# Decoder layer on one core: every SBUF tile starts on a multiple of 128 bytes

## Chip, core and metric

The kernel runs on one core of one Trainium2 chip. The metric is the device time of one execution in microseconds (us); what is compared is the median of several runs. TensorE (PE in the profile) does the matrix products, VectorE (DVE), ScalarE (ACT) and GpSimd (POOL) the elementwise work, and SyncE (SP) issues most of the transfers (DMA).

## The reference

One layer of a decoder, 1024 tokens by 1024 features, all in float32:

```
n   = RMSNorm(h)
c_q, c_kv, k_pe, q_sb, k_sb, v_sb, gate_a, gate_b = split(n @ w_in)
o_a = latent attention from c_q, c_kv, k_pe    (8 heads, rotary part, causal softmax)
o_b = stick-breaking attention(q_sb, k_sb, v_sb)                 (8 heads, causal)
h  += (sigmoid(gate_a) * (o_a @ w_br_mla) + sigmoid(gate_b) * (o_b @ w_br_sb)) @ w_out
n2  = RMSNorm(h)
h  += (silu(n2 @ w_ffn_gate) * (n2 @ w_ffn_up)) @ w_ffn_down     (inner width 2816)
h  += sigmoid(h @ w_ple_gate) * RMSNorm(p @ w_ple_proj)
out = RMSNorm(h)
```

## The kernel before

Each factor of a product is split into two float32r tiles, a high part and the rest (`split`, L115: a cast on ScalarE, a subtraction on VectorE), and a product is three passes, high by high, high by rest, rest by high (`passes`, L119 to L124). Each pass is one matmul with its own load of weights (PEld): `lhsT` is loaded as the weights, `rhs`, 512 columns of 2,048 bytes per partition, streams past them as the moving operand. The profile names a product by its PSUM tile:

- `nb` (L327): the value projection, up to 100 us. `pt` (L203, L354, L385, L393): query, key, low-rank and gate projections. Some stand in the first 100 us; the rest fill the stick-breaking attention (100 to 480 us) and are there till about 560.
- latent attention to 820 us; `pb` (L766) and `po` (L775), the merge and the output product, to about 960.
- `pP`, `pQ`, `pR` (L927): the gate and up products of the feed-forward, 22 units of seven products of 12 passes (a Strassen-like scheme, `wino`, L896), from about 960 to 1490 us. The work around a unit: SP loads `raw` (1 MB), POOL forms sums (L901, L902, L918, L920) and multiplies gate by up (L966), VectorE subtracts (L959), SP stores the results to DRAM (L956), loads four blocks of `w_ffn_down` into `t` tiles (L1077), VectorE adds them in pairs (L1080), SP stores the sums (L1081) and loads the next `raw`. SP issues in the order in which these stand. Two `embed` steps (L1028) lie between.
- `pd` (L1153): the down product, 1490 to 1710 us; `pg` (L1194): the last gate, then the output.

A scheduler sets the order of the instructions on each engine; a tile's slot is reused when its readers have finished.

**Where tiles lie.** SBUF pools are stacks, one from the left end, one from the right, and the framework gives each tile a whole number of 32-byte slots. The left stack begins on a multiple of 128 bytes; the small constants (L90 to L101) take 32 or 96 bytes each, in all a multiple of 128, so the large left tiles start on such a multiple, except those behind other small tiles. The right stack ends at 229,344 bytes, which is 96 past a multiple of 128, so its tiles start 96 bytes past one, or, below a pool with small tiles, 32. For the large products the start of the operands, modulo 128 bytes, is, read off the built program:

| product | weights | at | moving operand | at |
|---|---|---|---|---|
| nb | nTh, nTl | 96 | w_h, w_l | 32 |
| pt | w_h, w_l | 32 | nTh, nTl | 96 |
| pP, pQ, pR | wl (both parts) | 96 | b | 0 |
| pb (L766) | wh, wl | 96 | oh, ol | 96 |
| po | wo | 0 | mT | 0 |
| pd | dls | 32 | drs | 32 |
| pg | wpg | 0 | hs | 0 |

Every slice that a pass takes starts a multiple of 512 bytes into its tile, so these numbers hold for each pass.

Of the kernel before, what the change touches and what calls it, by code (L numbers as in the profile page):

```python
# [10 lines left out]
F32 = mybir.dt.float32  # L11
# [8 lines left out]
P = 128  # L20
S = 1024
D = 1024
NT = S // P
NK = D // P
# [27 lines left out]
def decoder_layer(ctx: ExitStack, tc: tile.TileContext, x, p, positions, g_mix, w_in, g_q_a, w_q_b,  # L52
                  g_kv_a, w_kv_b, w_br_mla, w_br_sb, w_out, g_ffn, w_ffn_gate, w_ffn_up, w_ffn_down,
                  w_ple_gate, w_ple_proj, g_ple, g_final, xT, pT, out):
    nc = tc.nc
# [6 lines left out]
    def pool(stack, name, side="left", space=None, bufs=1):  # L62
        kw = {} if space is None else {"space": space}
        if space is None:
            kw["side"] = side
        return stack.enter_context(tc.tile_pool(name=name, bufs=bufs, reuse_waits="tile", **kw))

    dram = ctx.enter_context(tc.tile_pool(name="dram", bufs=1, space=DRAM))
    d_c = dram.tile([Q_RANK + KV_RANK + 2 * ROPE, S], F32, name="d_c")
# [9 lines left out]
    d_rope = dram.tile([64, S], F32, name="d_rope")  # L79


    const = pool(ctx, "const", side="left")
    ident = const.tile([P, P], F32, name="ident")
    make_identity(nc, ident)
    atc = ExitStack()
    attc = pool(atc, "attconst")
    ident_r = attc.tile([P, P], F32R, name="ident_r")
    nc.vector.tensor_copy(out=ident_r, in_=ident)

    mhalf = const.tile([P, 1], F32, name="mhalf")  # L90
    nc.vector.memset(mhalf, -0.5)

    ones = const.tile([P, 1], F32, name="ones")
    nc.vector.memset(ones, 1.0)
    ones_pp = const.tile([P, P], F32, name="ones_pp")
    nc.vector.memset(ones_pp, 1.0)
    gains = const.tile([P, 3, NK], F32, name="gains")
    for gi, g in enumerate((g_ffn, g_ple, g_final)):
        nc.sync.dma_start(out=gains[:, gi, :], in_=g.rearrange("o (k p) -> p (o k)", p=P))
    r_ple = const.tile([P, NT], F32, name="r_ple")  # L100
    r_ffn = const.tile([P, NT], F32, name="r_ffn")  # L101
    incl = attc.tile([P, P], F32R, name="incl")
    rest = attc.tile([P, P], F32R, name="rest")
    mask_sb = attc.tile([P, P], F32R, name="mask_sb")
# [36 lines left out]
    late = ExitStack()  # L141
    with ExitStack() as att:
        ps = pool(ctx, "psum", space=PSUM)
        A = dict(tag="A", bufs=4)
        B = dict(tag="B", bufs=2)
# [14 lines left out]
        with ExitStack() as sb:  # L160
# [63 lines left out]
            with ExitStack() as p0:  # L224
# [13 lines left out]
                for t in range(NT):  # L238
# [8 lines left out]
                    for c in range(0, NK, 4):  # L247
                        tp = ps.tile([P, 512], F32, name="tp", **(B if c == 0 else A))
# [23 lines left out]
            with ExitStack() as p2:  # L272
                rp = pool(p2, "ropetab", side="left")

                HI = slice(64, 128)
                gcol = const.tile([P, 5], F32, name="gcol")
                nc.sync.dma_start(out=gcol[:, 0:3], in_=g_q_a.rearrange("o (k p) -> p (o k)", p=P))
                nc.sync.dma_start(out=gcol[:, 3:5], in_=g_kv_a.rearrange("o (k p) -> p (o k)", p=P))
                frow = rp.tile([1, 64], F32, name="frow")
                for i in range(16):  # L280
                    for j, sg in enumerate((1.0, 1.0, -1.0, 1.0)):
                        nc.gpsimd.memset(frow[0:1, 16 * j + i:16 * j + i + 1], sg * INV_FREQ[i])
                fcol = rp.tile([P, 2], F32, name="fcol")
                nc.sync.dma_start(out=d_freq, in_=frow)
                nc.sync.dma_start(out=fcol[HI, 0:1], in_=d_freq.rearrange("o f -> f o"))
                nc.gpsimd.memset(fcol[64:96, 1:2], math.pi / 2)
                nc.gpsimd.memset(fcol[96:128, 1:2], 0.0)
                pos_i = rp.tile([P, S], I32, name="pos_i")
                nc.sync.dma_start(out=pos_i[HI, :], in_=positions.broadcast_to([64, S]))
                ang = rp.tile([P, S], F32, name="ang")  # L290
                kk = rp.tile([P, S], F32, name="kk")
                kh = rp.tile([P, S], F32, name="kh")
                an, k_, h_ = ang[HI], kk[HI], kh[HI]
                V = nc.vector
                V.tensor_copy(out=k_, in_=pos_i[HI, :])
                V.tensor_scalar(out=an, in0=k_, scalar1=fcol[HI, 0:1], scalar2=None, op0=ALU.mult)
                V.tensor_scalar(out=k_, in0=an, scalar1=1.0 / (2 * math.pi), scalar2=None, op0=ALU.mult)
                V.tensor_scalar(out=k_, in0=k_, scalar1=MAGIC, scalar2=None, op0=ALU.add)
                V.tensor_scalar(out=k_, in0=k_, scalar1=-MAGIC, scalar2=None, op0=ALU.add)
                V.tensor_scalar(out=h_, in0=k_, scalar1=1.0 / 4096.0, scalar2=None, op0=ALU.mult)  # L300
                V.tensor_scalar(out=h_, in0=h_, scalar1=MAGIC, scalar2=None, op0=ALU.add)
                V.tensor_scalar(out=h_, in0=h_, scalar1=-MAGIC, scalar2=None, op0=ALU.add)
                V.scalar_tensor_tensor(out=k_, in0=h_, scalar=-4096.0, in1=k_, op0=ALU.mult, op1=ALU.add)
                for c in TWO_PI_PARTS:
                    V.scalar_tensor_tensor(out=an, in0=h_, scalar=-4096.0 * c, in1=an, op0=ALU.mult, op1=ALU.add)
                    V.scalar_tensor_tensor(out=an, in0=k_, scalar=-c, in1=an, op0=ALU.mult, op1=ALU.add)
                V.tensor_scalar(out=an, in0=an, scalar1=fcol[HI, 1:2], scalar2=None, op0=ALU.add)
                V.tensor_scalar(out=k_, in0=an, scalar1=math.pi, scalar2=-2.0 * math.pi, op0=ALU.is_gt, op1=ALU.mult)
                V.tensor_tensor(out=an, in0=an, in1=k_, op=ALU.add)
                V.tensor_scalar(out=an, in0=an, scalar1=PI_BELOW, scalar2=-PI_BELOW, op0=ALU.min, op1=ALU.max)  # L310
                nc.scalar.activation(out=an, in_=an, func=AF.Sin)
                nc.sync.dma_start(out=d_rope, in_=an)
# [171 lines left out]
        with ExitStack() as ml:  # L484
# [64 lines left out]
            for c in range(3):  # L549
                t = wk.tile([P, S], F32, name="cq", tag="pw1", bufs=4)  # L550
# [128 lines left out]
            for h in range(HEADS):  # L679
# [17 lines left out]
                if h == 5:  # L697
# [8 lines left out]
                        oa.append(hl)  # L706
                    oa.append([oah, oal])
    atc.close()

    bigs = itertools.cycle((M, A, A, A, A))  # L710

# [411 lines left out]
    for i in (1, 2, 6, 5, 7, 3, 4):  # L1123
# [31 lines left out]
        f, t = {1: (0, 0), 2: (0, 0), 6: (0, 1), 5: (1, 1), 7: (1, 1), 3: (0, 1), 4: (1, 0)}[i]  # L1155
# [93 lines left out]
```

## Time and profile before

| | |
|---|---|
| median of 3 runs | 1819.79 us (1817.94 to 1823.07) |
| the profiled execution's own time | 1825.25 us |
| its span, first to last instruction | 1823.5 us |
| PE busy | 1725.6 us (95%), 8148 matmuls |
| DVE, ACT, POOL busy | 1185.3, 907.0, 373.1 us (65%, 50%, 20%) |
| mean granted TensorE clock | 0.978 |
| chain that ended last, by engine | PE 70%, DVE 10%, DMA 7%, issue 6%, POOL 3%, ACT 2% |

Busy time of PE says little here: ends of matmuls are modelled, and one that lasts 0.39 us by the record overlaps the next. The spacing of their starts tells the pace. The chain is followed back from the last instruction, at each step to what released it; what an engine does beside the chain is hidden. The granted clock is 1.00 at 2.4 GHz and 0.5 at 1.2 GHz.

### The profile page before, as it was taken

How to read it: one execution, taken by the hardware profiler on the slowest of the kernel's cores; microseconds unless marked ns; L12 is line 12 of the kernel's file. 1: busy time of each engine (PE TensorE's matmuls, PEld its weight loads, DVE VectorE, ACT ScalarE, POOL GpSimd, SP SyncE). 2: the span in 40 equal slices, each digit the busy share in tenths (PEclk: the TensorE clock that was granted, in tenths of full speed). 3: DMA queues.
4: the chain of work that ended last, by engine and by line, in shares of the span. 5: the costliest groups of instructions: out<-in, count | busy, mean ns of one | idle time of the engine just before them, and what ended most of it. 6: DMA issues, size and time to landing. Idle time of an engine off the chain costs nothing.

```text
span 1823.5 us, 23396 instructions
## 1 busy us (share of the span) xinstructions
PE 1725.6 (95%) x8148; PEld 1416.5 (78%) x8148; DVE 1185.3 (65%) x2077; ACT 907.0 (50%) x1762; POOL 373.1 (20%) x401
## 2 busy tenths in 40 slices
PE   6999999999999999996997999989999999999996
PEld 5888878888787888875885777768778778887795
DVE  6666788777886667776569666654642455556655
ACT  5265677766765767765234433343333334445421
POOL 2011210000212433333104133324313410000000
PEclk9999999999999999998998999999998999999998
DMA  5212122213314111218840266464523328665522
GB/s 168 57 56 51 52 59 59 64 47 99 104 47 151 54 59 36 64 59 321 295 154 32 88 204 201 172 213 165 194 91 106 110 87 311 192 191 171 168 69 77
DMA packets 172345, 223.21 MB, mean 122 GB/s; under 512 B 23426, under 2 KB 104322, under 8 KB 172226
## 3 DMA queue, kind: packets, MB, share of 16 engines
q1 hardware_dynamic: 166194, 201.78, 34.4%
q0 software_dynamic: 6032, 19.93, 3.0%
q8 instruction: 64, 1.05, 0.3%
q14 instruction: 55, 0.45, 0.1%
HBM read 152.98 MB, written 67.90 MB: 121 GB/s over the span
## 4 chain that ended last, share of the span: by engine, by line
PE 70%; DVE 10%; DMA 7%; issue 6%; POOL 3%; ACT 2%; SPq 1%; DVEq 0%; POOLq 0%; ACTq 0%
PE pt L122 5%; PE pt L123 5%; PE pt L124 5%; PE pd L122 4%; PE pd L123 4%; PE pd L124 4%; DMA t<-w_ffn_down 2%; PE pP L124 2%; PE pP L122 2%; PE pP L123 2%; PE tp L636 2%; DVE t L959 2%; PE pg L124 1%; PE po L122 1%; PE pg L123 1%
## 5 line engine op out<-in xcount | busy, mean ns | idle before, releaser
L122 PE MATMUL pt<-nTh,w_h 128*128 128x512 f32 (+1 forms) x480 | 192.4, 402 | 3.3 <-ACT go L340 2.3
L117 DVE TENSOR_TENSOR wl<-raw,wl 128x512 fp32r<-128x512 f32 x132 | 112.1, 849 | 122.5 <-ACT wl L116 122.1
L123 PE MATMUL pt<-nTl,w_h 128*128 128x512 f32 (+1 forms) x480 | 190.2, 396 | 0.0
L124 PE MATMUL pt<-nTh,w_l 128*128 128x512 f32 (+1 forms) x480 | 189.5, 396 | 0.0
L124 PE MATMUL pP<-b,wl 128*128 128x512 f32 x352 | 142.5, 407 | 13.0 <-DVE wl L117 13.0
L116 ACT CAST wl<-raw 128x512 fp32r<-128x512 f32 x132 | 82.0, 621 | 138.3 <-PE pP L124 63.3
L122 PE MATMUL pP<-b,wl 128*128 128x512 f32 x352 | 143.3, 407 | 4.2 <-ACT wl L116 2.6
L123 PE MATMUL pP<-b,wl 128*128 128x512 f32 x352 | 142.1, 404 | 0.0
L122 PEld LDWEIGHTS pt<-nTh,w_h 128*128 128x128 f32 (+1 forms) x480 | 90.0, 188 | 26.1 <-ACT go L340 5.0
L124 PEld LDWEIGHTS pt<-nTh,w_l 128*128 128x128 f32 (+1 forms) x480 | 90.2, 188 | 20.4
L123 PEld LDWEIGHTS pt<-nTl,w_h 128*128 128x128 f32 (+1 forms) x480 | 90.2, 188 | 19.2
L123 PE MATMUL pd<-drs,dls 128*128 128x512 f32 x296 | 102.1, 389 | 1.0 <-DVE drs L117 1.0
L124 PE MATMUL pd<-drs,dls 128*128 128x512 f32 x296 | 102.0, 389 | 0.0
L117 DVE TENSOR_TENSOR drs<-drr,drs 128x512 fp32r<-128x512 f32 x74 | 50.9, 690 | 77.3 <-ACT drs L116 77.3
L122 PE MATMUL pd<-drs,dls 128*128 128x512 f32 x296 | 99.6, 392 | 0.4 <-ACT dls L116 0.4
L116 ACT CAST drs<-drr 128x512 fp32r<-128x512 f32 x74 | 45.9, 623 | 101.6 <-PE pd L124 99.1
L124 PEld LDWEIGHTS pP<-b,wl 128*128 128x128 f32 x352 | 68.2, 194 | 33.2 <-DVE wl L117 16.9
L622 POOL TENSOR_SCALAR pw<-pw,st 128x128 f32<-128x128 f32 (+5 forms) x48 | 74.9, 1567 | 71.7 <-DVE st L618 20.4
L122 PEld LDWEIGHTS pP<-b,wl 128*128 128x128 f32 x352 | 68.1, 194 | 22.6 <-ACT wl L116 4.1
L123 PEld LDWEIGHTS pP<-b,wl 128*128 128x128 f32 x352 | 67.7, 192 | 16.0
L430 DVE TENSOR_TENSOR sz<-sz,T 128x512 f32<-128x512 f32 (+2 forms) x96 | 52.2, 550 | 36.1 <-PE T L428 35.0
L122 PE MATMUL pQ<-b,wl 128*128 128x512 f32 x176 | 70.4, 401 | 1.3 <-ACT b L116 0.8
(373 smaller groups left out, 4793.6 us busy)
## 6 DMA issues: line engine op xcount, KB each, us to landing
d_g<-t SPq DMA_DIRECT2D x74, 256.0 KB, 2.1
drr<-d_g SPq DMA_DIRECT2D x74, 256.0 KB, 2.9
w_raw<-w_in SPq DMA_DIRECT2D x33, 512.0 KB, 4.3
raw<-w_ffn_gate SPq DMA_DIRECT2D x11, 1024.0 KB, 5.4
raw<-w_ffn_up SPq DMA_DIRECT2D x11, 1024.0 KB, 6.7
t<-w_ffn_down SPq DMA_DIRECT2D x44, 256.0 KB, 4.2
d_w<-t SPq DMA_DIRECT2D x44, 256.0 KB, 2.2
drr<-d_w SPq DMA_DIRECT2D x44, 256.0 KB, 2.7
```

Source lines behind the costliest of these rows:

```text
L116: nc.scalar.copy(out=h, in_=src)
L117: eng.tensor_tensor(out=l, in0=src, in1=r32(h), op=ALU.subtract)
L122: nc.tensor.matmul(ps, lhsT=ah, rhs=bh, start=first and i == 0, stop=False, **kw)
L123: nc.tensor.matmul(ps, lhsT=ah, rhs=bl, start=False, stop=False, **kw)
L124: nc.tensor.matmul(ps, lhsT=al, rhs=bh, start=False, stop=last and i == n - 1, **kw)
L430: nc.vector.tensor_tensor(out=sz[:, c0:], in0=sz[:, c0:], in1=T[:, c0:], op=ALU.subtract)
L622: nc.gpsimd.tensor_scalar(out=pw[:, 0:nk], in0=pw[:, 0:nk], scalar1=st[:, 6:7], scalar2=None, op0=ALU.mult)
L636: nc.tensor.transpose(tp[:, i * P:(i + 1) * P], rows[i][:, kb * P:(kb + 1) * P], ident)
L959: nc.vector.tensor_tensor(out=dst, in0=a, in1=b, op=ALU.subtract)
```

## The change

In every SBUF pool a tile whose bytes per partition are no multiple of 128 is padded to the next multiple (class `Lines`; the kernel works on the unpadded view). The small constants go into one tile `cols` of 256 bytes. A tile of 96 bytes, never used, is put at the right edge first, so that all later right-hand tiles start on a multiple of 128. `ones_pp`, the matrix of ones for the broadcasts of L721, moves from the constants to a pool that opens once the attention constants are closed, in the place of one of them.

```diff
-        return stack.enter_context(tc.tile_pool(name=name, bufs=bufs, reuse_waits="tile", **kw))
+        tp = stack.enter_context(tc.tile_pool(name=name, bufs=bufs, reuse_waits="tile", **kw))
+        return tp if space is not None else Lines(tp)
+
+    class Lines:
+
+
+        def __init__(self, tp):
+            self.tp = tp
+
+        def tile(self, shape, dtype, **kw):
+            n = shape[-1]
+            if math.prod(shape[1:]) % 32 == 0:
+                return self.tp.tile(shape, dtype, **kw)
+            t = self.tp.tile(list(shape[:-1]) + [-(-n // 32) * 32], dtype, **kw)
+            return t[..., 0:n] if len(shape) > 2 else t[:, 0:n]
...
+    edge = pool(ctx, "edge", side="right")
+    edge.tp.tile([P, 24], F32, name="edge")
     const = pool(ctx, "const", side="left")
...
-    mhalf = const.tile([P, 1], F32, name="mhalf")
+    cols = const.tile([P, 64], F32, name="cols")
+    mhalf = cols[:, 0:1]
     nc.vector.memset(mhalf, -0.5)
 
-    ones = const.tile([P, 1], F32, name="ones")
+    ones = cols[:, 1:2]
     nc.vector.memset(ones, 1.0)
-    ones_pp = const.tile([P, P], F32, name="ones_pp")
-    nc.vector.memset(ones_pp, 1.0)
-    gains = const.tile([P, 3, NK], F32, name="gains")
+    gains = cols[:, 8:32].rearrange("p (a b) -> p a b", b=NK)
...
-    r_ple = const.tile([P, NT], F32, name="r_ple")
-    r_ffn = const.tile([P, NT], F32, name="r_ffn")
+    r_ple = cols[:, 32:40]
+    r_ffn = cols[:, 40:48]
...
-                gcol = const.tile([P, 5], F32, name="gcol")
+                gcol = cols[:, 48:53]
...
     atc.close()
+    ones_pp = pool(ctx, "ones").tile([P, P], F32, name="ones_pp")
+    nc.vector.memset(ones_pp, 1.0)
```

With it all the operands in the table above start at 0 modulo 128 bytes. The large tiles move by 512 bytes or less, some small ones by up to 416; after the attention stages the left-hand tiles lie where they lay. Line numbers shift, and on PE, ACT, POOL and SP the instructions stand in the same order as before. On VectorE one instruction moves. At the start of VectorE's list before (`ident_r`, `incl`, `rest` are attention constants):

```order
L91 MEMSET mhalf 128x1
L94 MEMSET ones 128x1
L96 MEMSET ones_pp 128x128
L88 CAST ident_r<-ident 128x128
L112 CAST incl<-tmpm 128x128
```

and after the change:

```order
L108 MEMSET cols 128x1
L111 MEMSET cols 128x1
L104 CAST ident_r<-ident 128x128
L127 CAST incl<-tmpm 128x128
L127 CAST rest<-tmpm 128x128
```

The fill of `ones_pp` is gone there. In the last head of the latent attention, where `sp` are scores, `st` softmax sums and `tl` the rest of the transposed weights, VectorE had before:

```order
L640 TENSOR_TENSOR tl<-tp,th 128x384
L609 TENSOR_TENSOR st<-st 128x1
L618 RECIPROCAL st<-st 128x1
L605 TENSOR_REDUCE st<-sp 128x1
L640 TENSOR_TENSOR tl<-tp,th 128x256
L609 TENSOR_TENSOR st<-st 128x1
```

and has after the change:

```order
L655 TENSOR_TENSOR tl<-tp,th 128x384
L624 TENSOR_TENSOR st<-st 128x1
L633 RECIPROCAL st<-st 128x1
L620 TENSOR_REDUCE st<-sp 128x1
L725 MEMSET ones_pp 128x128
L655 TENSOR_TENSOR tl<-tp,th 128x256
L624 TENSOR_TENSOR st<-st 128x1
```

The fill now stands behind the last row maximum.

## Rows read from the trace of the kernel before

**Rows 1.** The chain, shares by line, of 100 to 480 us.
```profile
by line: PE pt L122 22.5%; PE pt L123 21.8%; PE pt L124 21.6%; PE op L441 3.5%; PE op L439 3.5%; PE T L426 3.4%; PE T L428 3.4%; PE z L407 3.4%; PE z L408 3.3%; PE T L432 2.8%; PE T L434 2.7%; PE pt L366 0.9%; PE z L410 0.9%; ACT w_h L116 0
```
**Rows 2.** The same of 1020 to 1490, of 1060 to 1140, of 1426 to 1490.
```profile
by line: DMA t<-w_ffn_down 8.6%; PE pP L124 7.6%; PE pP L122 7.3%; PE pP L123 7.2%; DVE t L959 6.0%; issue 5.4%; POOL t L966 5.0%; DMA raw<-w_ffn_gate 4.7%; DMA raw<-w_ffn_up 4.1%; PE pQ L123 4.0%; PE pQ L122 4.0%; PE pQ L124 4.0%; PE pm L1
...
by line: DMA t<-w_ffn_down 22.8%; DMA raw<-w_ffn_up 16.1%; issue 10.5%; DVE t L959 8.8%; DMA raw<-w_ffn_gate 6.7%; DVE wl L117 6.5%; POOL t L966 6.4%; DVE t L1080 5.9%; SPq L1077 5.6%; POOL s L901 4.9%; POOL spare L966 2.2%; POOL raw L902 2
...
by line: PE pP L124 19.0%; PE pP L122 18.7%; PE pP L123 18.7%; PE pQ L124 10.3%; PE pQ L123 10.2%; PE pQ L122 10.2%; PE pR L124 4.4%; PE pR L123 4.4%; PE pR L122 4.4%
```
**Rows 3.** PE's waits, 1060 to 1360: us in total, times, longest.
```profile
PE pP L124 <- DVE wl L117: 9.5, 5, 3.1
```
**Rows 4.** Timeline of PE: start us, length us, instruction; first and last of six stretches.
```profile
45.55 0.39 PE L123 MATMUL pt<-nTl,w_h 128*128 128x512 f32 x1
55.86 0.39 PE L124 MATMUL pt<-nTh,w_l 128*128 128x512 f32 x1
56.09 0.39 PE L122 MATMUL nb<-w_h,nTh 128*128 128x512 f32 x1
97.39 0.40 PE L124 MATMUL nb<-w_h,nTl 128*128 128x512 f32 x1
854.38 0.40 PE L123 MATMUL po<-mT,wo 128*128 128x512 f32 x1
895.22 0.39 PE L124 MATMUL po<-mT,wo 128*128 128x512 f32 x1
895.45 0.40 PE L122 MATMUL pb<-oh,wh 128*128 128x512 f32 x1
917.03 0.40 PE L124 MATMUL pb<-oah,wl 128*128 128x512 f32 x1
1402.83 0.40 PE L122 MATMUL pP<-b,wl 128*128 128x512 f32 x1
1411.03 0.40 PE L124 MATMUL pP<-b,wl 128*128 128x512 f32 x1
1509.64 0.39 PE L123 MATMUL pd<-drs,dls 128*128 128x512 f32 x1
1610.06 0.39 PE L122 MATMUL pd<-drs,dls 128*128 128x512 f32 x1
```
**Rows 5.** Groups by line and shape: count, busy us, mean ns, idle before.
```profile
L122 PE MATMUL pt<-nTh,w_h 128*128 128x512 f32 x464 | 186.2, 402 | 3.3 <-ACT go L340 2.3 <-ACT w_h L116 0.5 <-ACT nTh L254 0.2
L122 PE MATMUL pP<-b,wl 128*128 128x512 f32 x352 | 143.3, 407 | 4.2 <-ACT wl L116 2.6 <-ACT t L908 1.4 <-DVE t L911 0.2
L122 PE MATMUL pQ<-b,wl 128*128 128x512 f32 x176 | 70.4, 401 | 1.3 <-ACT b L116 0.8 <-ACT wl L116 0.5
L122 PE MATMUL pR<-b,wl 128*128 128x512 f32 x88 | 35.7, 406 | 2.1 <-DVE spare L911 1.9 <-ACT wl L116 0.2
L122 PE MATMUL nb<-w_h,nTh 128*128 128x512 f32 x64 | 24.9, 394 | 0.0
```
**Rows 6.** The same view, VectorE and ScalarE.
```profile
L117 DVE TENSOR_TENSOR drs<-drr,drs 128x512 fp32r<-128x512 f32 x74 | 50.9, 690 | 77.3 <-ACT drs L116 77.3
L425 DVE TENSOR_TENSOR sl<-e,sh 128x512 fp32r<-128x512 f32 x48 | 32.9, 684 | 1.6 <-ACT sh L424 1.5
L116 ACT CAST drs<-drr 128x512 fp32r<-128x512 f32 x74 | 45.9, 623 | 101.6 <-PE pd L124 99.1 <-DMA drr<-d_g 2.4
L424 ACT CAST sh<-e 128x512 fp32r<-128x512 f32 x48 | 29.6, 617 | 18.7 <-PE T L432 8.9 <-DVE e L418 8.7 <-PE pt L122 0.6
```
**Rows 7.** Stretches: PE, PEld, DVE, ACT, POOL busy; clock, DMA share, GB/s.
```profile
1060.00:1160.00 100.00, 97.13 (x414) 77.51 (x413) 65.79 (x82) 33.44 (x58) 38.00 (x27) 1.00 0.61 202
1160.00:1180.00 20.00, 18.04 (x72) 14.08 (x71) 13.59 (x17) 5.91 (x11) 6.72 (x5) 0.91 0.54 189
1520.00:1540.00 20.00, 20.00 (x90) 16.56 (x89) 11.91 (x19) 8.24 (x14) 0.00 (x0) 1.00 0.95 344
880.00:900.00 20.00, 20.00 (x89) 16.52 (x88) 9.05 (x12) 2.00 (x2) 0.00 (x0) 1.00 0.73 257
```
**Rows 8.** One line's instructions: min, median, max ns, first and last start.
```profile
L96 DVE MEMSET ones_pp<- x1: 165/165/165, 1.0 to 1.0; 128x128 f32 x1
```

## The prediction

> **What bounds the kernel now.** I read the chain of waits first, stretch by stretch, because the change alters no operation and can only tell where an instruction's own pace changes. From 100 to 480 us the three passes of `pt` alone are 66% of the chain [rows 1]: TensorE sets the time there. In the gate and up stage it does so only in part. Over 1020 to 1490 us `pP` and `pQ` have 34% of the chain, with loads, stores and the elementwise steps between them [rows 2]. From 1060 to 1140 no TensorE line stands in the part of the row that is printed, which covers nearly all of the chain: there the end is set by a loop of `raw` load, POOL, VectorE subtraction, store, load of `w_ffn_down`, addition, next `raw`. From 1426 to 1490 the chain is TensorE alone. TensorE is still busy 97.1 of 100 us from 1060 to 1160 [rows 7], and its five waits for the weights' rest part in 1060 to 1360 sum to 9.5 us [rows 3]. So the loop and TensorE are nearly equal there, and the loop is slightly the longer.
>
> **Who feels a tile's start?** The kernel before has tiles at 0, 32 and 96 bytes past a multiple of 128, so its own trace holds the comparison. On VectorE a subtraction of 512 columns takes 690 ns with its tiles at 32 (`drs`) and 684 ns at 0 (`sl`); on ScalarE the cast takes 623 and 617 ns [rows 6]. Both pairs are within 1%, which I take as nothing. For transfers, bytes over busy share give 344/0.95 = 362 GB/s for the loads of 1520 to 1540, into tiles at 32, and 257/0.73 = 352 GB/s for 880 to 900, with tiles at 0 [rows 7]: no gain from a start at 0.
>
> TensorE is another matter. I divided the time between the first and the last start of long unbroken stretches by the number of passes begun between them [rows 4]:
>
> - weights and moving operand equally far past a multiple of 128: `po` (0 and 0) 40.84 us / 180 = 226.9 ns; `pb` (96 and 96) 21.58 / 95 = 227.2; `pd` (32 and 32) 100.42 / 443 = 226.7;
> - not equally far: `pt` (32 and 96) 10.31 / 45 = 229.1; `nb` (96 and 32) 41.30 / 177 = 233.3; `pP` (96 and 0) 8.20 / 35 = 234.3.
>
> All of them move 512 columns at granted clock 1.00, with the same three passes. The three equal pairs agree within 0.5 ns although VectorE, ScalarE and the transfers are busy in quite different shares. What separates the two lists is whether the two operands have the same start, not whether either lies at 0. After the change all are at 0 and 0, a pair that the trace shows at 226.9. So I take 226.7 for all.
>
> **The change part by part.**
>
> - *Gate and up products.* Counts are (352 + 176 + 88) x 3 = 1848 passes [rows 5]; each loses 234.3 - 226.7 = 7.6 ns, 14.0 us of TensorE's work. Off the end comes only what lies on the chain: 34% of 470 us is 160 us [rows 2], and 7.6/234.3 of it is 5.2 us. Where the loop has the chain, TensorE finishes sooner and waits longer for the same `wl`: the 9.5 us of waits [rows 3] grow and the end stays. That is what is late next. Bounds are 0 (the loop takes over everywhere) and 14.0 (the loop tightens as much as TensorE does); I take 5.2, which the chain says.
> - *`nb`.* 64 x 3 = 192 passes, 233.3 - 226.7 = 6.6 ns each: 1.3 us. They stand in one stretch without a wait (idle 0.0) [rows 5], so all of it counts.
> - *`pt`.* 464 x 3 = 1392 passes [rows 5] at 229.1 - 226.7 = 2.4 ns: 3.3 us at most. On the chain of 100 to 480 there are 66% of 380 us = 250 us [rows 1], and 2.4/229.1 of it is 2.6 us. In that stage `pt` passes alternate with those of the attention, so many have no long run in which to show the even pace; bounds 0 and 3.3, I take 2.4.
> - *The other products* (`po`, `pb`, `pd`, `pg`, latent attention) have equal starts already: nothing.
> - *The fill of `ones_pp`.* It costs 165 ns [rows 8] at 1.0 us, where VectorE waits for the first loads anyway, and will cost as much between two softmax steps of the last attention head, ahead of one `tl`. Behind it on VectorE are that `tl` and the product that waits for it: 0.2 us if nothing covers it. It needs no wait of its own, being queued behind the last row maximum, and its first reader is a `bc` product late in the merge. 0 to 0.2; I take 0.1 as loss.
> - *Padding and the shared `cols` tile.* The order on all other engines is unchanged and no instruction is added; nothing.
>
> The sum is 5.2 + 1.3 + 2.4 - 0.1 = 8.8 us. The profiled execution took 1825.25 us, so its like would take 1816.4. The runs shown have a median of 1819.79, 0.3% below that execution; taken off the median, the forecast is **1811 us**.
>
> **A rule that speaks against it.** [Rows 4] show the pace hanging on the operands' starts. The Trainium skill says otherwise: "SBUF — State Buffer", section "Specifications (TRN2)", has SBUF in lines of 16 bytes, so 32 and 96 are whole lines already, and its section "Who interferes with whom" gives TensorE independent read ports for weights and moving operand, and says that it never waits on anyone. By that rule the sum would be 0 and the time 1820 us; the trace disagrees with it by 2.4 to 7.6 ns a pass.
>
> [Rows 7] show transfers no slower into tiles at 32. The Trainium skill, "DMA: Bandwidth & Descriptors", section "How a descriptor splits into AXI transactions", lets a descriptor that starts off a 256-byte boundary pay for the bytes below it in beats of 32 bytes. By it a 2 KB row of `t`, which by the built program is stored from 224 past such a boundary, costs 7 beats more than its 64, and from 128, where the change puts it, 4: an estimate from that page of 4% of such a store. The trace shows no such difference, so the sum has none of it.
>
> **The rivals.**
>
> 1. *All of TensorE's saving comes through*, because the loop is itself paced by products that end sooner. For it: TensorE is busy 97% even where the loop has the chain. Against: the printed chain of 80 us there without a product. 14.0 + 1.3 + 3.3 = 18.6 us: 1801 us.
> 2. *The loop takes over the whole gate and up stage.* For it: five waits already. Against: 1426 to 1490 is TensorE alone. Only `nb` and `pt` remain, 3.7 us, less 0.1: 1816 us.
> 3. *The change does not do what it says for speed*: the slower paces belong to the stages (GpSimd is busy in one, the attention in the other), not to the starts. For it: no stage shows both a pair that is equal and one that is not. Against: `nb` runs at 233.3 ns in 41 us without a wait, at times when little else is busy, and `pb`, `po` keep 227 beside full transfers. 1820 us.
> 4. *Slower, by the clock.* In 1160 to 1180 the granted clock is 0.91 [rows 7]: a part of it ran at 1.2 GHz, behind one of the waits of rows 3. That is 9% of 20 us, 1.8 us. If faster products make the waits longer, and each of the five then brings two such drops where TensorE has no slack left for them, 5 x 2 x 1.8 = 18 us are added against 8.8 saved: 1829 us. It decides from the fifth drop on (9 us). Against: 1060 to 1160 holds waits too and keeps clock 1.00 [rows 7], and a longer wait is itself slack.
>
> **Chances and range.** The forecast 44%, rival 1 18%, rival 2 20%, rival 3 13%, rival 4 5%. Differences under 0.3%, 5.5 us, cannot be told from none here; the forecast's own spread, 1806 to 1815, lies nearly all below 1814.3. So faster by over 0.3% is 0.44 x 0.9 + 0.18 + a little of rival 2, 0.60; within 0.3% is 0.35; slower 0.05. The range reaches from rival 1 to rival 3 with the scatter of the runs: 1800 to 1821 us.
>
> **What would show it.** Right: in the profile after, the spacing of `pP`, `pQ`, `pR`, `nb` in unbroken stretches is 226.7 ns, of `pt` near it; VectorE, ScalarE and transfers keep their durations; the waits of TensorE for `wl` between 1060 and 1360 grow from 9.5 us to some 15; the 1426 to 1490 stretch shortens by 2 us; `pd` and `pg` keep their length. Wrong: if the spacing of `pP` stays at 234.3 the cause of the pace is not the start; if it falls and the waits do not grow, rival 1 holds; if it falls and the end does not move, the loop has the whole stage; if transfers get shorter, my reading of rows 7 was too coarse.

## Result and profile after

The changed kernel takes 1808.96 us (median of 6 runs, 1804.43 to 1813.05) against 1820.81 for the kernel before on the same chip: ratio 0.9936, 95% interval [0.9918, 0.9954], 11.9 us less. The forecast was 1811, range 1800 to 1821. The profiled execution took 1808.15 us with a span of 1806.4. Ratios, here and below, but not medians, leave out an execution more than 1.5% above the fastest of its kernel; there is one such, of 4,613 us, among the five of e7.

The page of after: busy times, and the chain that ended last by engine. TensorE has lost 22.6 us of busy time, VectorE 3; the split of the chain has not moved.

```profile
PE 1703.0 (94%) x8148; PEld 1411.8 (78%) x8148; DVE 1182.2 (65%) x2077; ACT 906.9 (50%) x1762; POOL 373.7 (21%) x401
...
PE 70%; DVE 10%; DMA 7%; issue 6%; POOL 3%; ACT 2%; SPq 1%; DVEq 0%; POOLq 0%; ACTq 0%
```

The timeline of PE after, first and last start of five of the stretches of [rows 4] (start us, length us, instruction):

```profile
43.38 0.39 PE L138 MATMUL pt<-nTl,w_h 128*128 128x512 f32 x1
53.58 0.39 PE L139 MATMUL pt<-nTh,w_l 128*128 128x512 f32 x1
53.81 0.39 PE L137 MATMUL nb<-w_h,nTh 128*128 128x512 f32 x1
93.93 0.39 PE L139 MATMUL nb<-w_h,nTl 128*128 128x512 f32 x1
849.43 0.40 PE L138 MATMUL po<-mT,wo 128*128 128x512 f32 x1
889.60 0.39 PE L139 MATMUL po<-mT,wo 128*128 128x512 f32 x1
889.83 0.39 PE L137 MATMUL pb<-oh,wh 128*128 128x512 f32 x1
911.36 0.39 PE L139 MATMUL pb<-oah,wl 128*128 128x512 f32 x1
1388.23 0.39 PE L137 MATMUL pP<-b,wl 128*128 128x512 f32 x1
1396.17 0.39 PE L139 MATMUL pP<-b,wl 128*128 128x512 f32 x1
```

With 45, 177, 177, 95 and 35 passes begun between them: `pt` 226.7 ns (before 229.1), `nb` 226.7 (233.3), `po` 226.9, `pb` 226.6, `pP` 226.9 from rows rounded to 10 ns (234.3). Over all gaps of 222 to 242 ns between passes of the same product the means are `pP` 227.1, `nb` 226.8, `pt` 227.9 (before 234.2, 233.3, 230.0). The slow pace is gone wherever it was.

PE's waits for the rest part of the weights, 1060 to 1360 us, as [rows 3], and then 960 to 1500:

```profile
PE pP L139 <- DVE wl L132: 12.2, 5, 3.6
...
PE pP L139 <- DVE wl L132: 17.2, 9, 3.6
```

They were 9.5 and 13.0 us: grown by 2.7 and 4.2. The chain of 100 to 480, of 1020 to 1470 and of 1060 to 1140, as [rows 1, 2]:

```profile
by line: PE pt L137 22.0%; PE pt L138 21.3%; PE pt L139 21.1%; PE op L456 3.5%; PE op L454 3.4%; PE z L422 3.4%; PE T L443 3.4%; PE T L441 3.4%; PE z L423 3.4%; PE T L447 2.8%; issue 2.7%; PE T L449 2.7%; PE pt L381 0.9%; PE z L425 0.9%; DV
...
by line: DMA t<-w_ffn_down 8.8%; PE pP L139 6.9%; PE pP L137 6.6%; PE pP L138 6.5%; DVE t L976 6.2%; issue 5.3%; DMA raw<-w_ffn_gate 5.2%; POOL t L983 5.1%; DMA raw<-w_ffn_up 4.2%; PE pQ L138 4.0%; PE pQ L137 4.0%; PE pQ L139 4.0%; DVE t L1
...
by line: DMA t<-w_ffn_down 23.1%; DMA raw<-w_ffn_up 15.9%; DVE t L976 8.8%; issue 8.3%; POOL t L983 8.1%; POOL s L918 7.5%; DMA raw<-w_ffn_gate 6.6%; DVE t L1097 6.0%; SPq L1094 5.6%; DMA d_w<-t 4.8%; POOL raw L919 3.7%; DVE wl L132 3.5%; S
```

The loop of loads and elementwise work sets the end in the same places, with a little more of the chain. The groups of [rows 6] and the stretches of [rows 7] (us, busy of PE, PEld, DVE, ACT, POOL, clock, DMA share, GB/s):

```profile
L132 DVE TENSOR_TENSOR drs<-drr,drs 128x512 fp32r<-128x512 f32 x74 | 50.9, 691 | 77.3 <-ACT drs L131 77.3
L440 DVE TENSOR_TENSOR sl<-e,sh 128x512 fp32r<-128x512 f32 x48 | 32.9, 686 | 1.7 <-ACT sh L439 1.5
...
L131 ACT CAST drs<-drr 128x512 fp32r<-128x512 f32 x74 | 46.0, 624 | 101.5 <-PE pd L139 99.0 <-DMA drr<-d_g 2.4
```
```profile
1060.00:1160.00 100.00, 92.95 (x401) 75.85 (x400) 68.07 (x83) 32.77 (x57) 39.54 (x28) 0.98 0.60 200
...
1503.00:1523.00 20.00, 20.00 (x90) 16.55 (x89) 11.95 (x19) 8.24 (x14) 0.00 (x0) 1.00 0.95 345
```

`drs` and its source moved from 32 to 0 modulo 128 bytes: the subtraction took 691 ns for 690, and loads into them run at 345 GB/s for 344. None of these felt the move. From 1060 to 1160 TensorE is busy 93.0 us for 97.1, but with 401 matmuls for 414, so the two windows do not hold the same work; the same work is compared further below.

### The profile page after: what moved, and what is told of

Read it like the earlier page. It is cut to its first block, busy times and chain, and to the rows that moved or that the text cites. A ratio compares the mean times of both kernels' runs of the same rounds, so it can differ in the third digit from the quotient of the medians.

```text
span 1806.4 us, 23396 instructions
## 1 busy us (share of the span) xinstructions
PE 1703.0 (94%) x8148; PEld 1411.8 (78%) x8148; DVE 1182.2 (65%) x2077; ACT 906.9 (50%) x1762; POOL 373.7 (21%) x401
## 4 chain that ended last, share of the span: by engine, by line
PE 70%; DVE 10%; DMA 7%; issue 6%; POOL 3%; ACT 2%; SPq 1%; DVEq 0%; POOLq 0%; ACTq 0%
PE pt L137 5%; PE pt L138 5%; PE pt L139 5%; PE pd L137 4%; PE pd L138 4%; PE pd L139 4%; DMA t<-w_ffn_down 2%; PE pP L139 2%; PE pP L137 2%; PE pP L138 2%; PE tp L651 2%; DVE t L976 2%; PE po L137 1%; PE pg L139 1%; PE pg L137 1%
## 5 line engine op out<-in xcount | busy, mean ns | idle before, releaser
L139 PE MATMUL pP<-b,wl 128*128 128x512 f32 x352 | 140.3, 401 | 17.2 <-DVE wl L132 17.2
L137 PE MATMUL pP<-b,wl 128*128 128x512 f32 x352 | 141.5, 402 | 4.5 <-ACT wl L131 2.6
L138 PE MATMUL pP<-b,wl 128*128 128x512 f32 x352 | 140.0, 398 | 0.0
L356 POOL DMA_DIRECT2D d_gate<-go x32 | 17.8, 556 | 260.9 <-ACT go L355 221.8
```

What stands on the lines that cost most here:

```text
L137: nc.tensor.matmul(ps, lhsT=ah, rhs=bh, start=first and i == 0, stop=False, **kw)
L138: nc.tensor.matmul(ps, lhsT=ah, rhs=bl, start=False, stop=False, **kw)
L139: nc.tensor.matmul(ps, lhsT=al, rhs=bh, start=False, stop=last and i == n - 1, **kw)
L356: nc.gpsimd.dma_start(out=dst, in_=go[0:rows, :])
```

## Experiments

In the table below a pace is the mean over gaps of 222 to 242 ns, "apart" is weights' start minus moving operand's start modulo 256 bytes, read off the built programs. That column was made after the trains of e5 had been seen. Times of kernels are compared by their ratios to the kernel before on the same chip.

| run | apart: gate/up, nb, pt | pP, nb, pt ns | first pP to first pd us | median us | ratio [95%] |
|---|---|---|---|---|---|
| e9 before | 96, 64, 192 | 234.3, 233.3, 229.8 | 523.4 | 1822.09 | 0.9997 [0.9985, 1.001] |
| e1 after | 0, 0, 0 | 227.1, 226.8, 228.0 | 517.6 | 1810.36 | 0.993 [0.9911, 0.9948] |
| e2 | 224, 0, 0 | 233.3, 226.9, 228.0 | 519.7 | 1816.73 | 0.997 [0.9956, 0.9985] |
| e3 | 0, 64, 192 | 227.1, 233.3, 229.7 | 515.0 | 1813.77 | 0.9946 [0.9931, 0.9961] |
| e4 | 0, 0, 0 | 227.2, 226.9, 227.8 | 516.5 | 1811.59 | 0.9934 [0.9915, 0.9952] |
| e6 | 224, 64, 192 | 233.2, 233.3, 229.6 | 519.7 | 1817.13 | 0.9972 [0.9957, 0.9987] |
| e10 | 96, 64, 192 | 234.3, 233.3, 229.7 | 525.8 | 1820.95 | 0.9992 [0.9979, 1.0005] |
| e11 | 128, 0, 0 | 232.7, 226.9, 227.9 | 519.3 | 1814.57 | 0.9958 [0.9941, 0.9975] |

### The same kernel, and one pair undone at a time

After once more, without an edit: 

> The changed kernel once more, as the measure for the others of this set. Every theory: 1809 us, 0.9936 of the kernel before (1820.8).

Measured 0.993: as expected. Then gate and up alone:

```diff
+    pool(gu, "off", side="right").tp.tile([P, 8], F32, name="off")
     wk = pool(gu, "gateup", side="right")
```

> The changed kernel with 32 bytes put in front of the gate and up stage's right-hand pool: wl starts 96 past a multiple of 128, b at 0, as before the change; nb, pt, pd keep equal starts. Theory (the pace hangs on whether weights and moving operand start equally far past a multiple of 128): pP, pQ, pR go back to 234.3 ns a pass, nb stays at 226.8, pt at 227.9, pd at 226.9. How much of it reaches the end: by my sum 5.2 us, so 1814.2; if all that nb and pt do not explain is the gate and up stage's (11.85 - 3.7), 8.2 us, so 1817.1; rival (the loop of loads and elementwise work sets that whole stage): 1809, no change; rival (all 14.0 us of TensorE's work counts there): 1823.

Only `pP`, `pQ`, `pR` slowed, to 233.3 ns (not 234.3), and the time rose by 6.4 us from e1. Neither "the loop has all of it" (0) nor "all of TensorE's work counts" (+14) fits; my 5.2 and the other 8.2 lie on both sides, and the intervals do not part them. And `nb` and `pt` alone:

```diff
+            pool(nx, "off", side="right").tp.tile([P, 16], F32, name="off")
             wp = pool(nx, "w_sb", side="right")
```

> The changed kernel with 64 bytes put between the pools of nT and of w_h and w_l: these start at 64, nTh and nTl at 0, a difference of 64 as before the change; gate and up keep 0 and 0. Theory: nb goes back to 233.3 ns and pt to 229 to 230, pP stays at 227; time 1809 + 1.3 + 2.4 = 1812.7, and this with the loss of the run that makes gate and up unequal adds up to the whole 11.85. Rival (64 is far enough from 0 for both, or the slower pace belonged to the stages): nb at 226.8, 1809.

`nb` is back at 233.3 ns, `pt` at 229.7, `pP` stays at 227.1, and 3.4 us are lost (3.7 expected): the pace goes with the operands' starts, stage by stage, not with the stage. The two ratios, 0.9946 and 0.993, have intervals of 0.0015 and 0.0019, so the medians alone do not tell this loss from none. The profiles do: from TensorE's first matmul to the one that starts at 480 us in the first profile of before, the five with these pairs unequal (before, e9, e10, e3, e6) take 469.2 to 469.6 us, and six with them equal (after, e1, e2, e4, e11, e12) 462.8 to 467.7, 3.5 us less on the mean.

### Whole lines, or equal starts?

```diff
-    edge = pool(ctx, "edge", side="right")
-    edge.tp.tile([P, 24], F32, name="edge")
+    lead = pool(ctx, "lead", side="left")
+    lead.tp.tile([P, 24], F32, name="lead")
```

> The changed kernel with its 96-byte pad moved from the right end to the left end: every large tile, left and right, then starts 96 past a multiple of 128, and none on whole lines of 128. Theory (only equal starts count): pP, nb, pd at 226.7 to 227.1, VectorE, ScalarE and transfers as after; 1809. Rival (tiles must lie on whole lines of 128 bytes for TensorE, the engines or the transfers): no pass at 227, 1820 or above.

With no large tile on a whole line of 128 bytes the kernel is as fast as after (0.9934). Whole lines are not what counts. The converse came later, after the trains: whole lines, but 128 bytes apart.

```diff
+    pool(gu, "off", side="right").tp.tile([P, 32], F32, name="off")
     wk = pool(gu, "gateup", side="right")
```

> The changed kernel with 128 bytes in front of the gate and up pool: wl and b both start on whole lines of 128 bytes, but their difference modulo 256 is 128. Theory (difference modulo 256, from the trains: 128 apart 232.2 ns): pP, pQ, pR at 232.2, time 1810.4 + 1848 x 5.4 ns x 0.55 = 1816, ratio 0.996. Rival (whole lines of 128 are enough, which is what the change makes sure of): 227.0, ratio 0.993.

The pace is 232.7 ns and the ratio 0.9958 for the 0.993 of e1, some 5 us of the gain, though every tile still lies on whole lines. One unbroken stretch of 35 passes of `pP` on PE's timeline in e4, and one in e11:

```profile
1390.88 0.39 PE L137 MATMUL pP<-b,wl 128*128 128x512 f32 x1
...
1398.82 0.39 PE L139 MATMUL pP<-b,wl 128*128 128x512 f32 x1
```
```profile
1392.19 0.39 PE L137 MATMUL pP<-b,wl 128*128 128x512 f32 x1
...
1400.33 0.39 PE L139 MATMUL pP<-b,wl 128*128 128x512 f32 x1
```

7.94/35 = 226.9 and 8.14/35 = 232.6 ns.

### The pace by itself

```python
for w, m in COMBOS if r == 0 else COMBOS[::-1]:     # w, m: bytes past a multiple of 256
    o = train(f"w{chr(65 + w // 16)}m{chr(65 + m // 16)}", 48, w, m)   # 48 passes
o = train("alt", 48, 0, 0, 96)
```

> Only TensorE: trains of 48 passes (weights 128x128, moving operand 128x512, float32r, the order high by high, high by rest, rest by high), one train for each pair of starts, each pair twice, the second time in reverse order; the layer is left out, and nothing else runs beside the trains but a copy at the end of each. Theory: equal starts (0 and 0, 16 and 16, 32 and 32, 64 and 64, 96 and 96) and those apart by 128 or 256 give 226.7 ns a pass; starts apart by 32, 64 or 96 give 229 to 234; apart by 16, 48, 80, 112, which the layer never has, the same or worse. Rival (whole lines of 128 for each operand by itself): 32 and 32, 64 and 64, 96 and 96 slow as well. Rival (the pace came from what runs beside it in the layer): 226.7 for every pair. In the train where the weights of the high part start at 0 and those of the rest at 96, moving operand at 0: one pass in three or two in three slow, which shows whether it is the load of a pass's own weights or of the next one's.

PE's timeline of this run: start, length, and in the tile's name the weights' start (w) and the moving operand's (m) in steps of 16 bytes, A for 0, B 16, C 32, E 64, G 96, I 128, M 192, Q 256, U 320. A train's pace is the time to the next train's start over 48. The first of the two trains of a pair is shown.

```profile
22.40 11.04 PE L73 MATMUL wAmA<-mv,wt 128*128 128x512 f32 x48
33.28 11.05 PE L73 MATMUL wBmA<-mv,wt 128*128 128x512 f32 x48
44.17 11.35 PE L73 MATMUL wCmA<-mv,wt 128*128 128x512 f32 x48
55.36 11.36 PE L73 MATMUL wDmA<-mv,wt 128*128 128x512 f32 x48
66.56 11.35 PE L73 MATMUL wEmA<-mv,wt 128*128 128x512 f32 x48
77.75 11.29 PE L73 MATMUL wFmA<-mv,wt 128*128 128x512 f32 x48
88.88 11.40 PE L73 MATMUL wGmA<-mv,wt 128*128 128x512 f32 x48
100.11 11.36 PE L73 MATMUL wHmA<-mv,wt 128*128 128x512 f32 x48
...
122.43 11.36 PE L73 MATMUL wAmC<-mv,wt 128*128 128x512 f32 x48
133.63 11.20 PE L73 MATMUL wAmD<-mv,wt 128*128 128x512 f32 x48
144.67 11.16 PE L73 MATMUL wAmE<-mv,wt 128*128 128x512 f32 x48
155.67 11.26 PE L73 MATMUL wAmF<-mv,wt 128*128 128x512 f32 x48
...
189.07 11.05 PE L73 MATMUL wCmC<-mv,wt 128*128 128x512 f32 x48
199.96 11.08 PE L73 MATMUL wEmE<-mv,wt 128*128 128x512 f32 x48
210.88 11.07 PE L73 MATMUL wGmG<-mv,wt 128*128 128x512 f32 x48
221.78 11.15 PE L73 MATMUL wCmG<-mv,wt 128*128 128x512 f32 x48
232.77 11.36 PE L73 MATMUL wGmC<-mv,wt 128*128 128x512 f32 x48
243.97 11.26 PE L73 MATMUL wBmB<-mv,wt 128*128 128x512 f32 x48
255.07 11.30 PE L73 MATMUL wImA<-mv,wt 128*128 128x512 f32 x48
266.21 11.15 PE L73 MATMUL wMmA<-mv,wt 128*128 128x512 f32 x48
277.19 11.04 PE L73 MATMUL wQmA<-mv,wt 128*128 128x512 f32 x48
288.07 11.36 PE L73 MATMUL wUmA<-mv,wt 128*128 128x512 f32 x48
299.27 11.31 PE L73 MATMUL alt<-mv,wt 128*128 128x512 f32 x48
```

Equal starts of 0 give 10.88/48 = 226.7 ns, of 96 (`wGmG`) 227.1; 256 apart (`wQmA`) 226.7. But 128 apart (`wImA`) is 232.1, so my expectation for 128 was wrong. What orders the trains, for starts that are multiples of 32, is the difference modulo 256 (both trains of each pair):

| apart mod 256 | trains | ns | in the layer |
|---|---|---|---|
| 0 | 0/0, 32/32, 64/64, 96/96, 256/0 | 226.7 to 227.5 | after: all; before: po, pb, pd |
| 32 | 32/0 | 233.1 to 233.4 | |
| 64 | 64/0, 96/32, 320/0 | 233.1 to 233.3 | before: nb 233.3 |
| 96 | 96/0 | 234.0 to 234.4 | before: pP 234.3 |
| 128 | 128/0 | 232.1 to 232.5 | e11: pP 232.7 |
| 160 | 0/96 | 233.3 to 233.6 | |
| 192 | 0/64, 32/96, 192/0 | 228.8 to 229.3 | before: pt 229.1 |
| 224 | 0/32 | 233.3 | e2: pP 233.3 |

So it is neither whole lines nor the layer's other work: nothing runs beside these trains but a copy at the end of each, and they repeat the layer's paces. In `alt` all three passes were slow alike (about 232), so it does not tell whether a pass's own weights or the next one's meet the moving operand; that stays open. What in the engine makes the difference of the starts count, no run shows.

### Are the pairs all of it?

Both pads of e2 and e3 together:

> The changed kernel with both pads, in front of w_h and w_l (64 bytes) and in front of the gate and up pool (32 bytes): every pair of starts that the change made equal is unequal again, while the padded small tiles, the shared cols tile and the later fill of ones_pp stay. Theory (the pairs of starts are all that the change does for time): as the kernel before, ratio 1.000. Rival (the two losses add up and the rest of the gain, 12.75 - 6.4 - 3.4 = 3 us, belongs to the other parts): ratio 0.998.

0.9972 was nearer the rival: 5 us seemed to belong to something else. But gate and up were 224 apart here and ran at 233.2 ns, not 234.2. With 160 bytes in place of 32 they are 96 apart, as before:

```diff
-    pool(gu, "off", side="right").tp.tile([P, 8], F32, name="off")
+    pool(gu, "off", side="right").tp.tile([P, 40], F32, name="off")
```

> The changed kernel with 64 bytes in front of w_h and w_l and 160 bytes in front of the gate and up pool: weights minus moving operand, modulo 256, is then 192 for pt, 64 for nb and 96 for pP, pQ, pR, exactly as in the kernel before (the run with both pairs unequal had 224 for gate and up); everything else is as after. Theory (the pace hangs on that difference modulo 256): pP at 234.2 where the other had 233.3, pt 229.7, nb 233.3. Theory (the pairs are all that counts): ratio 1.000 to 0.999. Rival (other parts of the change give some 0.15 to 0.3%): 0.997 to 0.9985.

The paces are those of before (e9), and the ratio is 0.9992 [0.9979, 1.0005]: the padding, the shared `cols` tile and the late fill give nothing that can be told from none (the interval would hide up to 3.8 us). Between e6 and e10 lie 1.0 ns a pass, 1.9 us of TensorE, and 0.0020, 3.6 us, with intervals of 0.0015 and 0.0013; whether the rest of it is more than scatter stays open. One thing the profile of e10 has and that of e6 has not is a stretch at 1.2 GHz in the second embed step, which the first profile of before also shows:

> The kernel before once more, for a second profile of it. Ratio 1.000, 1822. What is open: in the first profile TensorE runs at 1.2 GHz from 1370 to 1380 us, in the second embed step, behind a wait of 1.9 us, and the profiles of the changed kernel and of five variants do not; between 1360 and 1381 they gain 4.7 us on it. Theory (a drop that one execution has and another not): this profile lacks it, or has one elsewhere. Rival (a step of the change shortens the waits in that embed step each time): it is there again.

Stretches behind the embed's waits, in the first profile of before, its second, and e10 (the clock is the third number from the end):

```profile
1370.00:1380.00 10.00, 10.00 (x33) 8.46 (x33) 4.32 (x3) 3.71 (x7) 4.49 (x3) 0.50 0.20 76
```
```profile
1372.00:1382.00 10.00, 10.00 (x60) 8.79 (x61) 4.34 (x3) 5.52 (x11) 4.19 (x3) 1.00 0.25 93
```
```profile
1367.00:1377.00 10.00, 10.00 (x34) 8.50 (x33) 4.01 (x3) 3.29 (x7) 4.01 (x3) 0.52 0.16 59
```

One execution of the kernel before has the drop and the other has not, so it does not come each time. It is most of why the two spans differ by 17.1 us where the medians differ by 11.9: 4.7 us are this one drop. Whether the change makes it rarer is not shown. Two of the three profiles with gate and up 96 apart have it, behind waits of `pp` of 1.9 and 2.6 us; none of the other ten has. e9 and e11 waited 1.8 us there without a drop, after, e1, e3 and e4 1.0 to 1.2. Over all executions the mean granted clock is 0.978 for before and for after.

### What keeps part of it from the end

TensorE begins the same 8148 matmuls in the same order in each of these runs, so that a stretch can be timed between the same two. One pair in the first profile of before, and the same in that of after:

```profile
1060.14 0.40 PE L123 MATMUL pP<-b,wl 128*128 128x512 f32 x1
1360.09 0.39 PE L123 MATMUL pP<-b,wl 128*128 128x512 f32 x1
```
```profile
1052.29 0.39 PE L138 MATMUL pP<-b,wl 128*128 128x512 f32 x1
1350.53 0.39 PE L138 MATMUL pP<-b,wl 128*128 128x512 f32 x1
```

299.9 and 298.2 us. The whole stage, cut at the matmuls that start at these times in the first profile of before; the last column is the mean of the first group less that of the third, and what 7.2 ns on each pass of `pP`, `pQ`, `pR` there would make:

| stretch | 234 ns: before, e9, e10 | 233 ns: e2, e6, e11 | 227 ns: after, e1, e3, e4 | came through, of us |
|---|---|---|---|---|
| 965 to 1060 | 95.0, 94.7, 94.3 | 94.2, 94.2, 94.3 | 92.9, 94.1, 92.9, 91.5 | 1.9 of 2.1 |
| 1060 to 1360, the loop | 299.9, 302.3, 299.5 | 299.3, 299.2, 299.0 | 298.2, 299.8, 298.0, 300.5 | 1.4 of 7.9 |
| 1360 to 1381, second embed | 21.0, 16.0, 21.5 | 16.2, 16.3, 16.2 | 16.2, 16.1, 16.5, 17.0 | 3.0 of 0.1 |
| 1381 to 1491 | 110.1, 110.1, 110.2 | 109.7, 109.8, 109.6 | 107.5, 107.3, 107.3, 107.2 | 2.8 of 3.1 |

Where the loop has much of the chain, what came through is no more than two profiles of one kernel differ by (299.9 and 302.3). The rest of the 7.9 us is in view: on the mean the four at 227 ns wait 20.7 us there for the 16.5 of the three at 234, and have 30 passes at 1.2 GHz for 21, at 0.2 us each 1.8 us. In the stretches before it and at the stage's end nearly all came through. The 3.0 us of the embed step are the drop to 1.2 GHz in two of the three profiles. The runs at 233 ns have no drop, and their stage is 3.5 us longer than at 227 ns, with none of it in the loop's stretch.

The sums of `w_ffn_down` left out of the loop, with equal starts and with those of e2:

```diff
-        if n < KK:
+        if n < 0:
             down_sums(n)
...
-                lw = raw_in(d_w[LEFT[i], kk])
+                lw = raw_in(down_block(0, 0, kk))
```

> The changed kernel without the sums of w_ffn_down in the gate and up stage (no loads of the four blocks, no VectorE additions, no stores; the down product reads blocks of w_ffn_down in their place): the loop beside TensorE is lightened. Theory (the loop sets part of that stage): TensorE's waits of 17 us for wl shrink to a few, and the time falls by 10 to 15 us, to about 1797. Rival (TensorE sets the stage, the waits are the clock's or the products' own): waits stay, 1809.

> The kernel without the sums, with gate and up starts unequal (96 and 0). Theory (what kept part of TensorE's gain in gate and up from the end is the loop): with the loop lightened the whole comes through, 1848 passes x 6.3 ns = 11.6 us above the kernel without the sums and equal starts. Rival (about half comes through whatever the loop does): 6.4 us above it.

Medians 1792.37 (0.9832 [0.9808, 0.9856]) and 1799.58 (0.9872 [0.9848, 0.9896]). PE's waits for `wl`, 960 to 1475 us, in the first of the two:

```profile
PE pP L139 <- DVE wl L132: 7.2, 9, 1.7
```

The lighter loop gives 18 us, more than the 10 to 15 expected, and takes 10 off that wait: the loop does set part of the stage. But the faster pace is worth 7.3 us there, no more than with the whole loop; with an interval of 4.4 us either way on each of the two, 11.6 and 6.4 are not told apart. The two profiles do not decide it: the stage takes 500.5 and 504.2 us, but with 46 and 20 passes at 1.2 GHz, some 5 us at 0.2 each. Last, one of the four sums on GpSimd:

```diff
-            nc.vector.tensor_tensor(out=a[dst], in0=a[x], in1=a[y], op=op)
+            (nc.gpsimd if i == 3 else nc.vector).tensor_tensor(out=a[dst], in0=a[x], in1=a[y], op=op)
```

> The changed kernel with one of the four sums of w_ffn_down blocks per step (the last) added by GpSimd, not VectorE: 11 additions of 0.7 to 1.7 us leave VectorE, which the split of wl waits behind. If VectorE's share sets the loop: TensorE's 17 us of waits for wl fall by 5, time 1803 to 1806, ratio 0.990. Rival (GpSimd is as much part of the loop, its raw sums come later by its 1.3 to 1.7 us): same or up to 8 us slower.

1810.34, 0.9935 [0.9922, 0.9949]: as after. The waits fell to 14.4 us and the time did not. No version beat the changed kernel with the whole layer computed.

## Why the prediction held, and where not

- **Who feels a start.** Right in kind: TensorE alone of what was compared, by the pair, not by each operand ([rows 6, 7] against the rows above; e3, e4). The subtraction of `wl`, whose tile moved from 96 to 0, takes 837 ns for 849, and 825 to 856 over ten profiles in no order of starts. Wrong in the rule: "the same start" modulo 128 was read from pairs that happened to be 0 or not 0 modulo 256 too. e11 has equal starts modulo 128 and runs at 232.7. That after the change every pair is equal modulo 256 as well, on which the whole forecast rests, was luck. The rule also left unexplained why `pt` lost 2.4 and `pP` 7.6 ns; they lie 192 and 96 bytes apart, and the trains have the same paces there. By the Trainium skill, "SBUF — State Buffer", section "Specifications (TRN2)", whose lines are 16 bytes, starts at 32 and 96 are whole lines; that does not account for the trains' 233 ns at 32 apart.
- **Transfers.** [Rows 7] are of loads, and their "0" modulo 128 is 128 modulo 256, so they do not test the prediction's estimate of 4% for stores of `t`. Those took 2.1 us (results) and 2.2 us (sums) from issue to landing, before and after alike; 4% would be 0.09 us, as fine as the view prints.
- **`nb` and `pt`.** 1.3 + 2.4 = 3.7 us forecast; e3 against e1 measures 3.4, and the first 480 us of the profiles 3.5. The paces fell by the amounts forecast. Held.
- **Gate and up.** This term was mis-sized: 5.2 us forecast. By the medians after gains 11.9 to 12.8 us on before; less 3.4 that is 8.5 to 9.4. The stage from the first `pP` to the first `pd` takes 525.1 us at 234 ns (mean of both profiles of before and e10: 526.3, 523.4, 525.8) and 516.0 at 227 (after, e1, e3, e4: 515.1, 517.6, 515.0, 516.5): 9.1 us of 1848 x 7.2 ns = 13.3, 68% for the chain's 34%. But the stretches show that the chain's share was near the mark for the pace itself: without the embed step 6.1 us came through, 1.4 of 7.9 in the loop and 4.7 of 5.2 outside it. At 233 ns it was 3.5 of some 11 us by the profiles, and 6.4 (e2) by the medians. What the sum had at nothing is the clock: some 3.0 of the 9.1 us are the drop in the second embed step, which [rows 7] do not show. Whether the kernel before has it as often as two times in three, and so how much of the 8.5 to 9.4 us it makes, stays open.
- **The waits.** Right in direction: 9.5 grew to 12.2 from 1060 to 1360, not to 15 (9.5, 9.4, 9.2 in before, e9, e10; 12.2, 13.7, 11.7, 13.1 in after, e1, e3, e4). Over the stage the waits for `wl` of `pP` and `pR` are 16.4 us in the three profiles at 234 ns and 19.9 in the four at 227 (+3.5), those for `wpj` 6.4 and 8.1 (+1.7). With 5.2 of 14.0 us coming through the prediction left 8.8 to be waited; these two grew by 5.2, and in the loop's stretch passes at 1.2 GHz took 1.8 more. The stretch at the stage's end shortened as forecast: from 1429.6 to 1493.8 us of before, TensorE gained 2.0 us on it.
- **The fill of `ones_pp`** takes 165 ns at 794.6 us, and nobody is shown to wait for it. `pd` (218.3 us from first to last start) and `pg` (94.7) kept their length to 0.1 us.
- **The rivals.** All of TensorE's saving (18.6 us): no. The loop has the whole stage (3.7): no, e2; but from 1060 to 1360 it nearly has. The pace belongs to the stages: no, e3 and e5. Slower by the clock: no; the two large drops found, of some 5 us each, are in profiles with the slow pace.

The gain of 8.8 us was 3 to 4 us too small, nearly all of it in the gate and up term; the interval of the first comparison, 8.4 to 14.9 us, just includes it, and the time lies in the range because that allows for as much scatter.

## What to carry to other kernels

Where an unbroken row of passes runs slower than another of the same shape, compare the starts of weights and moving operand: here, on starts that are multiples of 32, 512 columns took 226.7 to 227.5 ns when the two lay a multiple of 256 bytes apart and 229 to 234 otherwise. A pad of some bytes in front of one pool sets that, and padding each tile to 128 bytes does so only by luck. On a stage in which a loop beside TensorE has part of the chain, time its stretches between the same instructions: here 1.4 of 7.9 us came through in the loop and 4.7 of 5.2 outside it. And profile the kernel before more than once: one drop of the clock, 4.7 us in one execution, was nearly the size of the 5.2 us that were forecast for the stage.

## Not expected of the hardware

The period is 256 bytes, not 128: 256 apart ran at 226.7 ns, 128 apart at 232.1. Starts of 16 bytes are no better when equal: `wBmB` ran at 231.3 ns, where 226.7 was expected. With weights 16 bytes past a moving operand at 0, the first train ran at 226.9 and the second, in reverse order, at 233.3, so at steps of 16 the difference alone does not settle the pace; the pairs in steps of 32 repeated to 0.5 ns.
